# Hybrid short-convolution and RWKV-7 layer on one core: another planner for the instruction order, and rows scaled inside their transposing product

## The chip, the cores and the metric

One core of one Trainium2 chip. The metric is the device time of one execution in microseconds (us). Engines: PE (TensorE, with its weight loads shown apart as PEld), DVE (VectorE), ACT (ScalarE), POOL (GpSimd) and SP (SyncE, used here to issue DMAs). Each engine works through its own queue in order.

## The reference

One layer on 2048 prompt tokens and 8 x 8 sample tokens, with 1024 columns in float32:

```python
xn = rms_norm(x, norm_g)                 # x * rsqrt(mean(x*x) + eps) * g
p = xn @ w_in
pc, pr = p[..., :CONV_COLS], p[..., CONV_COLS:]
# conv branch: u = C*h, width-3 causal conv, y_conv = B * z * silu(G)
pr = pr + mu_shift * (pr_prev - pr)      # token shift; r, k, v, wl, al, gr are its columns
# per head: S_t = S_{t-1} diag(w_t) + (S_{t-1} (-kk_t)) (kk_t*a_t)^T + v_t k_t^T ;  o_t = S_t r_t
new_shift = xn[:, -1]
y = jnp.concatenate([y_conv, y_rwkv], axis=-1) @ w_out
return x + y, new_conv, new_shift, s_fin   # a final RMSNorm follows
```

Outputs are the normalised rows, the last two conv rows, the last normalised input row of each sequence (`shift_p`, `shift_s`) and the 64 x 64 state of each of the 8 heads.

## The kernel before

The 2048 prompt tokens are worked through in two halves of 1024 tokens (the sample tokens ride with the first). A half is cut into three blocks of 256, 384 and 384 tokens; the first block of the first half has 330 columns because of the sample tokens. Eight heads make four pairs, so there are eight steps, s = 0 to 7, in the loop behind L930: half and pair are `divmod(s, 4)`.

`xprep` (L211) prepares a half. It loads rows of 128 tokens, squares them on ACT for the sum, takes a reciprocal root on DVE, and multiplies each row by its factor and by the norm weight in one DVE instruction (`stt`, L120, with `grow`, the weight spread over all partitions). The third row tile of blocks 1 and 2 takes ACT and POOL (L265) instead. Then PE transposes 128 x 128 squares (L286; the sample rows in L279), and each result is split into a rounded part `xh` (ACT) and the rest `xl` (DVE, L207). `xprep(0)` stands at the head, `xprep(1)` in step 3. The rows of outputs `shift_s` and `shift_p` are stored from the scaled rows.

`project` makes the columns of one weight tile for all three blocks: per block 24 matmuls (8 slices of 128, each as wh·xh, wh·xl, wl·xh) into a PSUM tile "pj", of which there are two, then an evacuation by ACT or DVE. In the first half the weights are split by ACT and POOL and saved to DRAM (`wsp`), in the second they are loaded from there by POOL's queue.

A step has these stages. `rwkv_pair` projects k, r, v and the gate and derives from them, by products with constant matrices (PSUM tiles "ax") and DVE work, the per-chunk operands L, bk, AB. `inverse` (L640) inverts the 64 x 64 triangular matrices of all 16 chunks: a substitution of 31 dependent DVE pairs, a transposition through DRAM, then back substitution with 32 x 32 matmuls (PSUM tile "cx") between DVE and ACT copies into `na` (L680, L687). `wkv` then runs 16 chunks of 64 tokens one after the other. Per chunk, `ca` gets L times the state `sv`; DVE copies it to `xs` (L741); `ca` gets AB times xs; DVE scales it to `u` (L751); `cb` gets bt times u; and DVE forms the next state `sv` from cb (L120). Beside the chain, "oo" collects the output. `conv_group` has four projections of its own and the convolution. After the steps, `out_tile` multiplies 17 row tiles by the output weights (48 matmuls each into pj).

Which instruction stands where in each engine's queue is not written in the code: the Tile scheduler takes the program, with its order as priority, through a model of the machine, and lets each engine take the first ready instruction of the model. So the projections of `conv_group` and of the next step fill the places where the chain waits in that model. Tile pools limit how far it goes ahead: two pj tiles, two of each weight tile, four of hp, seven of t. Once made, the order is fixed: an engine whose next instruction waits does not pass it.

Of the kernel before, what the change touches and what calls it, by code (L numbers as in the profile page):

```python
# [36 lines left out]
C_MASK, C_SMASK, C_SCM, C_SCS, C_BM = 0, 128, 256, 640, 704  # L37
NMASK = 712

P_MU, P_KK, P_KA, P_RK, P_LG, P_LB, P_W0, P_A0, P_CW = 0, 17, 21, 25, 29, 33, 37, 41, 45  # L40
NPRM = 57


def constants():
# [43 lines left out]
def trunk_kernel(ctx, tc, I, O):  # L88
# [27 lines left out]
    def copy(out, in_, scale=1.0, bias=0.0):  # L116
        act.activation(out=out, in_=in_, func=AF.Copy, scale=scale, bias=bias)  # L117

    def stt(out, in0, scalar, in1, op0=ALU.mult, op1=ALU.mult, eng=dve):
        eng.scalar_tensor_tensor(out=out, in0=in0, scalar=scalar, in1=in1, op0=op0, op1=op1)  # L120
# [23 lines left out]
    def rowtile():  # L144
        return T("half", [128, HALF + SAMP], "la0", 1)[:, :D]
# [59 lines left out]
    def split(hi, lo, src, eng=dve):  # L205
        copy(hi, src)
        eng.tensor_tensor(out=lo, in0=src, in1=hi.bitcast(F32), op=ALU.subtract)  # L207
# [1 line left out]
    WR = T("w", [128, KT, 128], "wr", 1)  # L209

    def xprep(hf):  # L211
        grow = rowtile()
        if hf == 1:
            act.dma_start(out=grow, in_=I["norm_g"].partition_broadcast(128).rearrange("p a d -> p (a d)"))
        if hf == 0:
            act.dma_start(out=cst[:, 0:128], in_=I["consts"][:, 0:128])
        xh, xl = [], []
        stage = [0]

        def staging():  # L220
            stage[0] += 1
            if stage[0] == (5, 3)[hf] or stage[0] == 11:
                return T("half", [128, HALF + SAMP], "la1", 1)[:, :D]
            if stage[0] == 5:
                return WR.rearrange("p k c -> p (k c)")
            if stage[0] == 6 and hf == 0:
                return T("pair", [128, 32, 32], "na", 1).rearrange("p a b -> p (a b)")
            return T("half", [128, 1108], "hp", 4)[:, :D]

        for bl in half_blocks(hf):  # L230
            h = T("xn", [128, KT, bl.cols], f"xh{bl.i}", 1, F32R)
            l = T("xn", [128, KT, bl.cols], f"xl{bl.i}", 1, F32R)
            xh.append(h)
            xl.append(l)
            rows = []
            if bl.samp:
                rows.append((I["x_sample"], SAMP, bl.c0 + 128))
            for i in range(bl.np // 128):
                tok = hf * HALF + bl.p0 + i * 128
                rows.append((I["x_prompt"][tok:tok + 128, :], 128, bl.c0 + i * 128))  # L240
            ss = T("small", [128, 3], "ssx", 2)[:, :len(rows)]
            if bl.samp:
                pool.memset(ss, 1.0)
            xts = []
            for j, (src, n, o) in enumerate(rows):
                xt = staging()[:n]
                sync.dma_start(out=xt, in_=src)
                junk = l[:n, :, o:o + 128]
                if hf == 1:
                    junk = T("ch", [128, KT, 128], "c2", 4, BF16)  # L250
                act.activation(out=junk, in_=xt.rearrange("p (k c) -> p k c", k=KT), func=AF.Square,
                               accum_out=ss[:n, j:j + 1])
                xts.append(xt)
            if bl.samp:
                sync.dma_start(out=grow, in_=I["norm_g"].partition_broadcast(128).rearrange("p a d -> p (a d)"))
                sr = T("small", [128, 144], "sub", 1)[:, :KT * NB].rearrange("p (k b) -> p k b", k=KT)
                act.dma_start(out=sr, in_=I["state_shift"])
                load_params()
            dve.tensor_scalar(out=ss, in0=ss, scalar1=1.0 / D, scalar2=RMS_EPS, op0=ALU.mult, op1=ALU.add)
            r = rsqrt(ss, len(rows), 128, "n")  # L260
            for j, xt in enumerate(xts):
                n = rows[j][1]
                if bl.i and j == 2:
                    copy(xt, xt, scale=r[:n, j:j + 1])
                    pool.tensor_tensor(out=xt, in0=xt, in1=grow[:n], op=ALU.mult)  # L265
                else:
                    stt(xt, xt, r[:n, j:j + 1], grow[:n])
            if bl.samp:
                pool.memset(h[:, :, 72:74].bitcast(F32), 0.0)
                pool.memset(l[:, :, 72:74].bitcast(F32), 0.0)  # L270
                hv = h[:, :, 0:72].rearrange("p k (b j) -> p k b j", j=9)
                lv = l[:, :, 0:72].rearrange("p k (b j) -> p k b j", j=9)
                split(hv[:, :, :, 0], lv[:, :, :, 0], sr)
                xt = xts.pop(0)
                rows.pop(0)
                pool.dma_start(out=O["shift_s"], in_=xt[7:SAMP:8, :])
                ps = AX([128, KT, SAMP])
                for k in range(KT):
                    pe.transpose(out=ps[:, k, :], in_=xt[:, k * 128:(k + 1) * 128], identity=ident[:SAMP, :SAMP])  # L279
                split(hv[:, :, :, 1:9], lv[:, :, :, 1:9], ps.rearrange("p k (b j) -> p k b j", j=8))  # L280
            for xt, (_, _, o) in zip(xts, rows):
                for q in range(2):
                    ps = AX([128, 4, 128])
                    for k in range(4):
                        kk = q * 4 + k
                        pe.transpose(out=ps[:, k, :], in_=xt[:, kk * 128:(kk + 1) * 128], identity=ident)  # L286
                    split(h[:, q * 4:q * 4 + 4, o:o + 128], l[:, q * 4:q * 4 + 4, o:o + 128], ps)
            if hf == 1 and bl.i == 2:
                act.dma_start(out=O["shift_p"], in_=xts[-1][127:128, :])
        return xh, xl  # L290

    wsp = dram.tile([33, 2, 128, KT, 128], F32, name="wsp")

# [638 lines left out]
    for s in range(8):  # L932
        hf, p = divmod(s, NPAIR)
        first = []
        if p == 0:
            la = [T("half", [128, HALF + SAMP], f"la{i}", 1, F32R) for i in range(2)]

            def la_block(bl):
                t = tmp()[:, :bl.nt]
                ts = slice(bl.t0, bl.t0 + bl.nt)  # L940

                def after():
                    act.activation(out=t[0:64], in_=t[0:64], func=AF.Tanh)
                    for i, hs in heads():
                        hi, lo = la[i][hs, ts], la[i][64 - 64 * i:128 - 64 * i, ts]
                        copy(hi, t[hs])
                        dve.tensor_tensor(out=lo, in0=t[hs], in1=hi.bitcast(F32), op=ALU.subtract)

                return t, after

            first.append((CONV_COLS + 3 * CW, shifter(hf, 12, la_block)))
            if s == 0:
                load_masks()
        S = Pair(hf, p)
        run(rwkv_pair(S, xs, la, *first))
        if s == 3:
            run(conv_group(xs, hf, p))
            xs = xprep(1)
        run(inverse(S))
        wkv(S)  # L960
        if s != 3:
            run(conv_group(xs, hf, p))
# [17 lines left out]
def layout(inputs):  # L980

    import numpy as np

    def cols(name):
        return np.asarray(inputs[name]).reshape(-1, 128).T

    a = {n: np.asarray(inputs[n]) for n in inputs}
    r = {
        "consts": constants()[0],
        "masks": constants()[1],  # L990
        "params": np.concatenate([cols(n) for n in ("mu_shift", "k_k", "k_a", "r_k", "lnx_g", "lnx_b", "w0", "a0",
                                                    "conv_w")], axis=1),
        "w_da": np.concatenate([np.tile(a[n][0].reshape(64, NPAIR, 128).transpose(1, 0, 2), (1, 2, 1))
                                for n in ("w_dec2", "w_a2")], axis=2),
        "state_conv": a["state_conv"].reshape(NB * 2, 4, 128).transpose(2, 1, 0),
        "state_shift": a["state_shift"].reshape(NB, KT, 128).transpose(2, 1, 0),
        "state_wkv": a["state_wkv"].reshape(NB, NPAIR, 2, HD, HD).transpose(1, 2, 4, 0, 3).reshape(
            NPAIR, 128, NB, HD),
        "w_in": a["w_in"].reshape(KT, 128, -1, 128).transpose(2, 1, 0, 3),
        "w_out": a["w_out"][0],  # L1000
        "norm_g": a["norm_g"],
        "final_norm_g": a["final_norm_g"],
        "x_prompt": a["x_prompt"][0],
        "x_sample": a["x_sample"].reshape(SAMP, D),
    }
    return {n: np.ascontiguousarray(v) for n, v in r.items()}
# [22 lines left out]
```

## Time and profile before

| | us |
|---|---|
| median of 3 runs | 1621.16 |
| lowest and highest run | 1619.57, 1629.75 |
| profiled execution, its own time | 1613.0 |
| its span in the profile | 1610.9 |
| PE busy in it | 1512.1 |

The mean granted PE clock of that execution is 0.969 of full speed. The profile is a record of that one execution: start and duration of instructions on every engine, inferred releasers of waits, and the granted clock. A row of the timeline may join several records (x4); a matmul of two heads stands as x2 or x4. "Idle before" is the engine's time without work ahead of that instruction. [...]

### The profile page before, as it was taken

The page shows a single profiled execution, that of the slowest core. Times are in us where ns is not written, and L with a number is a line of the kernel's source. Part 1 is how long each engine was busy: PE and PEld are TensorE (multiplying, and loading weights), DVE is VectorE, ACT ScalarE, POOL GpSimd, SP SyncE. Part 2 cuts the span into 40 slices and gives each one's busy share as a digit, 9 for nine tenths or more (in the row PEclk, how much of TensorE's full clock was granted, in tenths as well). Part 3 has the DMA queues.
Part 4 walks back from the last instruction along what each step waited for, and adds up shares of the span by engine and source line. Part 5 has one row for each costly group of instructions (what it writes and reads, how often), then busy time and mean ns, then how long its engine had stood idle before and what let it go on. Part 6 is the DMA issues. An engine that isn't in the chain of part 4 may idle for free.

```text
span 1610.9 us, 29335 instructions
## 1 busy us (share of the span) xinstructions
PE 1512.1 (94%) x11088; PEld 1265.4 (79%) x11088; DVE 1011.3 (63%) x3101; ACT 616.2 (38%) x1591; POOL 289.6 (18%) x395
## 2 busy tenths in 40 slices
PE   4999999999999999989999999999999999899997
PEld 4989778887788777877789678877897788567885
DVE  6377458765687458784586358545864578466544
ACT  6443346324542354344541354135313543342221
POOL 3134103311133112320022002200220022000000
PEclk9989999899999998999999899999999999899999
DMA  7323412342043213441124112411241145414441
GB/s 241 118 83 110 137 49 74 108 122 78 20 136 113 95 50 112 140 125 61 36 73 125 42 36 66 135 39 37 77 127 38 34 118 155 133 62 137 143 137 53
DMA packets 121967, 151.90 MB, mean 94 GB/s; under 512 B 62617, under 2 KB 86681, under 8 KB 121826
## 3 DMA queue, kind: packets, MB, share of 16 engines
q1 hardware_dynamic: 107024, 104.53, 21.2%
q0 software_dynamic: 9536, 34.64, 6.8%
q10 hardware_dynamic: 5266, 10.86, 1.9%
q8 instruction: 88, 1.44, 0.4%
q14 instruction: 53, 0.43, 0.1%
HBM read 92.60 MB, written 57.35 MB: 93 GB/s over the span
## 4 chain that ended last, share of the span: by engine, by line
PE 63%; DVE 23%; issue 5%; DMA 5%; ACT 2%; POOL 1%; SPq 1%; ACTq 0%; DVEq 0%; POOLq 0%
PE pj L129 41%; PE ca L129 5%; PE ax L129 5%; DVE sub L123 5%; PE cb L129 4%; DVE xi L123 4%; DVE hp L123 2%; PE oo L129 2%; PE cx L129 2%; DVE hp L120 1%; PE cx L703 1%; DVE bk L123 1%; DVE t L120 1%; DMA dx<-xi 1%; DMA AB<-dx 1%
## 5 line engine op out<-in xcount | busy, mean ns | idle before, releaser
L129 PE MATMUL pj<-xh,wh 128*128 128x384 f32 (+3 forms) x1856 | 655.4, 354 | 18.0 <-DVE hp L123 13.8
L129 PE MATMUL pj<-xl,wh 128*128 128x384 f32 (+3 forms) x1856 | 652.8, 352 | 2.7 <-POOL xl L207 2.1
L129 PE MATMUL pj<-xh,wl 128*128 128x384 f32 (+3 forms) x1856 | 650.9, 351 | 0.8 <-DMA wl<-wsp 0.8
L129 PEld LDWEIGHTS pj<-xh,wh 128*128 128x128 f32 x1856 | 356.7, 192 | 50.1 <-DVE hp L123 11.5
L129 PEld LDWEIGHTS pj<-xl,wh 128*128 128x128 f32 x1856 | 356.8, 192 | 31.7 <-POOL xl L207 3.0
L129 PEld LDWEIGHTS pj<-xh,wl 128*128 128x128 f32 x1856 | 355.8, 192 | 27.3 <-issue 1.7
L117 ACT ACTIVATE tS<-sv,wc 64x64 f32<-64x64 f32 x256 | 88.0, 344 | 114.8 <-DVE sv L120 94.2
L207 POOL TENSOR_TENSOR wl<-wr,wh 128x512 fp32r<-128x512 f32 x66 | 87.8, 1342 | 193.4 <-ACT wh L117 190.0
L120 DVE SCALAR_TENSOR_TENSOR sv<-cb,wc,tS 64x64 f32<-64x64 f32 x240 | 68.0, 283 | 62.6 <-PE cb L129 56.1
L129 PE MATMUL ax<-L,bk 64*128 64x128 f32 x528 | 79.1, 298 | 20.9 <-DVE bk L123 11.2
L129 PEld LDWEIGHTS ax<-L,bk 64*128 64x128 f32 x528 | 66.1, 197 | 37.9 <-issue 23.6
L123 DVE TENSOR_TENSOR sub<-xi,na 128x126 f32<-128x126 f32 (+22 forms) x248 | 81.5, 329 | 16.5 <-DMA na<-dn 9.7
L117 ACT ACTIVATE t<-pj,prm 128x384 f32<-128x384 f32 (+3 forms) x170 | 68.8, 433 | 54.5 <-PE pj L129 53.4
L751 DVE TENSOR_SCALAR u<-ca,Q 128x64 f32<-128x64 f32 x128 | 36.2, 283 | 82.3 <-PE ca L129 82.1
L531 POOL TENSOR_TENSOR bk<-t,t 64x384 f32<-64x384 f32 (+2 forms) x56 | 58.3, 1041 | 155.3 <-ACT t L503 72.9
L123 DVE TENSOR_TENSOR xi<-xi,sub 128x126 f32<-128x126 f32 (+22 forms) x248 | 77.6, 313 | 7.1
L117 ACT ACTIVATE wh<-wr 128x512 fp32r<-128x512 f32 x66 | 40.5, 626 | 92.0 <-PE pj L129 73.1
L129 PEld LDWEIGHTS ca<-sv,L 128*64 128x64 f32 x528 | 43.3, 134 | 37.2 <-DVE sv L120 12.8
L129 PE MATMUL ca<-sv,L 128*64 128x64 f32 x528 | 67.8, 245 | 0.1
L741 DVE COPY xs<-ca 128x64 f32<-128x64 f32 x128 | 28.7, 224 | 60.4 <-PE ca L129 50.6
L298 POOL DMA_DIRECT2D wh<-wsp x33 | 18.6, 565 | 254.1 <-PE pj L129 216.7
L123 DVE TENSOR_TENSOR hp<-pj,hp 128x512 f32<-128x512 f32 (+1 forms) x34 | 23.4, 689 | 62.6 <-PE pj L129 62.2
(207 smaller groups left out, 2057.4 us busy)
## 6 DMA issues: line engine op xcount, KB each, us to landing
wr<-in_w_in SPq DMA_DIRECT2D x66, 256.0 KB, 3.7
wsp<-wh SPq DMA_DIRECT2D x33, 512.0 KB, 3.1
wsp<-wl SPq DMA_DIRECT2D x33, 512.0 KB, 3.5
wh<-wsp POOLq DMA_DIRECT2D x33, 512.0 KB, 3.6
wl<-wsp POOLq DMA_DIRECT2D x33, 512.0 KB, 4.8
hp<-in_x_prompt SPq DMA_DIRECT2D x28, 512.0 KB, 4.1
la<-yd SPq DMA_DIRECT2D x16, 512.0 KB, 4.0
out_y_p<-hp ACTq DMA_DIRECT2D x16, 512.0 KB, 2.6
```

Of the source, the lines that this page charges most:

```text
L117: act.activation(out=out, in_=in_, func=AF.Copy, scale=scale, bias=bias)
L120: eng.scalar_tensor_tensor(out=out, in0=in0, scalar=scalar, in1=in1, op0=op0, op1=op1)
L123: dve.tensor_tensor(out=out, in0=in0, in1=in1, op=op)
L129: pe.matmul(out, lhsT=lhsT, rhs=rhs, start=start, stop=stop)
L207: eng.tensor_tensor(out=lo, in0=src, in1=hi.bitcast(F32), op=ALU.subtract)
L298: pool.dma_start(out=wh, in_=wsp[col, 0])
L531: pool.tensor_tensor(out=S.bk[bl.i][hs, chs, h, :], in0=ta[hs, a:a + n].rearrange("p (c j) -> p c j", j=64), in1=wi[hs, a:a + n].rearrange ...
L703: pe.transpose(out=pb[:, i, :], in_=S.bk[bi][:, ca + i].rearrange("p a t -> p (a t)"), identity=ident)
L741: dve.tensor_copy(out=xs_, in_=px)
L751: dve.tensor_scalar(out=u, in0=pu, scalar1=S.Q[:, q:q + 1], scalar2=None, op0=ALU.mult)
```

## The change

It has three parts. First, the Tile context gets `schedule_with_timeline_sim=True`: the scheduler's model of the machine is its detailed timing model, and the order on every engine comes out another way. Second, `xprep` no longer scales rows. DVE makes a diagonal matrix `dg` of the row factors (identity times r, 128 x 128 per row tile), and PE multiplies the row tile, as stationary operand, with it, slice by slice for all row tiles of a block. The product is the transposed, scaled slice. The norm weight, now one value per partition (8 more columns of the parameters, `P_NG`), is applied as ACT rounds to `xh` and as DVE forms `xl`. Third, `shift_rows`, called in step 0, loads the nine rows that the two shift outputs need and normalises them apart.

```diff
-NPRM = 57
+NPRM = 65
...
     def xprep(hf):
-        grow = rowtile()
...
             r = rsqrt(ss, len(rows), 128, "n")
-            for j, xt in enumerate(xts):
-                n = rows[j][1]
-                if bl.i and j == 2:
-                    copy(xt, xt, scale=r[:n, j:j + 1])
-                    pool.tensor_tensor(out=xt, in0=xt, in1=grow[:n], op=ALU.mult)
-                else:
-                    stt(xt, xt, r[:n, j:j + 1], grow[:n])
+            dg = tmp()
+            offs, o = [], 0
+            for j, (_, n, _) in enumerate(rows):
+                dve.tensor_scalar(out=dg[:n, o:o + n], in0=ident[:n, :n], scalar1=r[:n, j:j + 1], scalar2=None,
+                                  op0=ALU.mult)
+                offs.append((o, n))
+                o += n
...
-            for xt, (_, _, o) in zip(xts, rows):
-                for q in range(2):
-                    ps = AX([128, 4, 128])
-                    for k in range(4):
-                        kk = q * 4 + k
-                        pe.transpose(out=ps[:, k, :], in_=xt[:, kk * 128:(kk + 1) * 128], identity=ident)
-                    split(h[:, q * 4:q * 4 + 4, o:o + 128], l[:, q * 4:q * 4 + 4, o:o + 128], ps)
+            for k in range(KT):
+                tag, nb = (("ax", 2), ("ax", 2), ("cx", 1), ("oo", 1))[k % (4 if hf == 0 else 3)]
+                ps = PS([128, bl.np], tag, nb)
+                for i, (xt, (o, n)) in enumerate(zip(xts, offs)):
+                    mm(ps[:, i * 128:(i + 1) * 128], xt[:, k * 128:(k + 1) * 128], dg[:, o:o + n])
+                hk = h[:, k, bl.c0:bl.c0 + bl.np]
+                copy(hk, ps, scale=pcol(P_NG, k))
+                stt(l[:, k, bl.c0:bl.c0 + bl.np], ps, pcol(P_NG, k), hk.bitcast(F32), ALU.mult, ALU.subtract)
         return xh, xl
+
+    def shift_rows():
...
+        sync.dma_start(out=xt[0:NB], in_=I["x_sample"][7:SAMP:8, :])
+        sync.dma_start(out=xt[NB:n], in_=I["x_prompt"][SEQ - 1:SEQ, :])
...
+        act.activation(out=junk, in_=xt, func=AF.Square, accum_out=s)
+        dve.tensor_scalar(out=s, in0=s, scalar1=1.0 / D, scalar2=RMS_EPS, op0=ALU.mult, op1=ALU.add)
+        r = rsqrt(s, 1, n)
+        for q in range(2):
+            m = slice(q * 512, (q + 1) * 512)
+            g = T("ch", [128, 512], "c2", 4)[:n]
+            sync.dma_start(out=g, in_=I["norm_g"].partition_broadcast(n).rearrange("p a d -> p (a d)")[:, m])
+            stt(xt[:, m], xt[:, m], r, g)
+        act.dma_start(out=O["shift_s"], in_=xt[0:NB])
+        act.dma_start(out=O["shift_p"], in_=xt[NB:n])
...
-    with tile.TileContext(nc) as tc:
+    with tile.TileContext(nc, schedule_with_timeline_sim=True) as tc:
         trunk_kernel(tc, I, O)
```

The order on PE in one chunk of `wkv`, in step 5, before (ca, cb and oo are the chain's PSUM tiles, sv the state, bt and AB its operands, pj_12202 a projection of 256 columns):

```order
L129 MATMUL cb_11167<-sv_11149,bt_11148 64x64 x2
L129 MATMUL pj_12202<-xl_1193_7387,wh_12198 128x256
L129 MATMUL pj_12202<-xh_1192_7386,wl_12199 128x256
L129 MATMUL ca_11166<-xs_11250,AB_1738_10345 64x64 x2
L129 MATMUL pj_12202<-xh_1192_7386,wh_12198 128x256
L129 MATMUL pj_12202<-xl_1193_7387,wh_12198 128x256
L129 MATMUL pj_12202<-xh_1192_7386,wl_12199 128x256
L129 MATMUL pj_12202<-xh_1192_7386,wh_12198 128x256
L129 MATMUL cb_11167<-u_11259,bt_11148 64x64 x2
L129 MATMUL oo_11165<-u_11259,AB_1738_10345 64x64 x2
```

Every link here has projections behind it: two before the product of xs, four before that of u. A chunk of step 5 on PE after the change:

```order
L129 MATMUL ca_11386<-sv_11306,L_1761_10414 64x64
L129 MATMUL oo_11384<-sv_11306,L_1761_10414 64x64
L129 MATMUL ca_11386<-sv_11306,L_1764_10417 64x64
L129 MATMUL oo_11384<-sv_11306,L_1764_10417 64x64
L129 MATMUL cb_11387<-sv_11306,bt_11305 64x64 x2
L129 MATMUL ca_11386<-xs_11413,AB_1767_10420 64x64 x2
L129 MATMUL cb_11387<-u_11422,bt_11305 64x64 x2
L129 MATMUL oo_11384<-u_11422,AB_1767_10420 64x64 x2
```

A whole chunk, from the state sv to oo from u, now stands without a projection; they have moved to other chunks and out of the chain.

The second place is on PE in the back substitution of step 5, before (each cx of x12 is one product for the six chunks of block 1, the first operand of the next comes from DVE and ACT):

```order
L129 MATMUL pj_12142<-xl_1206_7442,wh_12107 128x384
L129 MATMUL cx_11082<-na_11049,AB_1739_10346 32x32 x12
L129 MATMUL pj_12142<-xh_1205_7441,wl_12108 128x384
L129 MATMUL pj_12142<-xh_1205_7441,wh_12107 128x384
L129 MATMUL pj_12142<-xl_1206_7442,wh_12107 128x384
L129 MATMUL pj_12142<-xh_1205_7441,wl_12108 128x384
L129 MATMUL pj_12142<-xh_1205_7441,wh_12107 128x384
L129 MATMUL cx_11097<-AB_1739_10346,na_11049 32x32 x12
L129 MATMUL pj_12142<-xl_1206_7442,wh_12107 128x384
```

Five pj stand between the first and the second product. The same place on PE after the change (pj_12402 is a projection of the first block, 256 columns):

```order
L129 MATMUL cx_11156<-na_11123,AB_1767_10420 32x32 x12
L129 MATMUL pj_12402<-xh_1209_7436,wh_12367 128x256
L129 MATMUL pj_12402<-xl_1210_7437,wh_12367 128x256
L129 MATMUL cx_11171<-AB_1767_10420,na_11123 32x32 x12
L129 MATMUL pj_12402<-xh_1209_7436,wl_12368 128x256
L129 MATMUL pj_12402<-xh_1209_7436,wh_12367 128x256
L129 MATMUL pj_12402<-xl_1210_7437,wh_12367 128x256
```

The projections between the first and the second product of this block are two instead of five; behind the second there are 22 in a row before the next product, where before there were five between each and the next.

## Rows read from the trace of the kernel before

**Rows 1.** Page, parts 1 and 2: busy time by engine, PE's forty slices

```profile
PE 1512.1 (94%) x11088; PEld 1265.4 (79%) x11088; DVE 1011.3 (63%) x3101; ACT 616.2 (38%) x1591; POOL 289.6 (18%) x395
...
PE   4999999999999999989999999999999999899997
```

**Rows 2.** Windows: span, PE busy (x count), granted clock, DMA share, GB/s

```profile
961.95:1063.03 101.08, 94.02 (x687) 0.97 0.30 85
1063.03:1120.28 57.25, 57.25 (x532) 1.00 0.13 44
1120.28:1225.10 104.82, 96.68 (x699) 0.95 0.31 85
```

**Rows 3.** Windows, the chunk chain, instructions of tile pj alone

```profile
1063.03:1120.28 57.25, 35.26 (x150) 1.00 0.13 44
```

**Rows 4.** Timeline, a filled chunk: start us, us, engine, line, operation

```profile
1093.45 0.60 DVE L120 SCALAR_TENSOR_TENSOR sv<-cb,wc,tS 64x64 f32<-64x64 f32 x2 [0.77 <-PE cb L129]
...
1093.93 0.33 PE L129 MATMUL ca<-sv,L 128*64 128x64 f32 x2
...
1095.84 0.34 PE L129 MATMUL pj<-xh,wh 128*128 128x384 f32 x1
1096.01 0.33 PE L129 MATMUL pj<-xl,wh 128*128 128x384 f32 x1
...
1096.73 0.60 DVE L120 SCALAR_TENSOR_TENSOR sv<-cb,wc,tS 64x64 f32<-64x64 f32 x2 [0.77 <-PE cb L129]
```

**Rows 5.** Timeline, a chunk with little beside it

```profile
227.07 0.60 DVE L120 SCALAR_TENSOR_TENSOR sv<-cb,wc,tS 64x64 f32<-64x64 f32 x2 [0.89 <-PE cb L129]
...
227.65 0.41 PE L129 MATMUL ca<-sv,L 128*64 128x64 f32 x3
...
228.16 0.22 DVE L741 COPY xs<-ca 128x64 f32<-128x64 f32 x1 [0.48 <-PE ca L129]
...
228.43 0.33 PE L703 MATMUL cx<-cst,bk 128*128 128x128 f32 x1
...
228.69 0.33 PE L129 MATMUL ca<-xs,AB 64*64 64x64 f32 x4
...
229.07 0.28 DVE L751 TENSOR_SCALAR u<-ca,Q 128x64 f32<-128x64 f32 x1 [0.69 <-PE ca L129]
...
229.58 0.33 PE L129 MATMUL cb<-u,bt 64*64 64x64 f32 x4
...
229.75 0.28 PE L129 MATMUL oo<-u,AB 64*64 64x64 f32 x4
...
230.03 0.60 DVE L120 SCALAR_TENSOR_TENSOR sv<-cb,wc,tS 64x64 f32<-64x64 f32 x2 [0.68 <-PE cb L129]
```

**Rows 6.** Waits of PE: total us, times, longest us

```profile
PE cx L129 <- DVE na L680: 14.6, 6, 5.2
PE pj L129 <- DVE hp L123: 13.8, 11, 2.5
```

**Rows 7.** Windows, columns as in rows 2, around a fall of the clock

```profile
276.00:281.60 5.60, 4.07 (x30) 1.00 0.61 209
281.60:292.00 10.40, 10.01 (x33) 0.53 0.34 113
292.00:302.00 10.00, 10.00 (x62) 0.97 0.02 3
```

**Rows 8.** Timeline of PE, six records at either clock level

```profile
286.04 1.65 PE L129 MATMUL ax<-L,bk 64*128 64x128 f32 x6
...
303.18 0.90 PE L129 MATMUL ax<-L,bk 64*128 64x128 f32 x6 [0.84 <-DVE L L123]
```

**Rows 9.** Costliest groups of the head, 0 to 40 us: busy us, mean ns, idle before

```profile
L120 DVE SCALAR_TENSOR_TENSOR hp<-hp,nwyn,la 128x1024 f32<-128x1024 f32 x5 | 8.2, 1660 | 0.1
```

**Rows 10.** Instructions of line L286: ns min/median/max, first and last start us

```profile
L286 PE MATMUL ax<-cst,wr x8: 270/272/273, 709.1 to 710.1; 128*128 128x128 f32 x8
```

**Rows 11.** Windows of the head, columns as in rows 2

```profile
0.00:40.00 40.00, 20.07 (x104) 1.00 0.72 243
```

More of the change, by code (lines that the diff above doesn't have):

```diff
@@ L38 @@
 NMASK = 712
-P_MU, P_KK, P_KA, P_RK, P_LG, P_LB, P_W0, P_A0, P_CW = 0, 17, 21, 25, 29, 33, 37, 41, 45
-NPRM = 57
+P_MU, P_KK, P_KA, P_RK, P_LG, P_LB, P_W0, P_A0, P_CW, P_NG = 0, 17, 21, 25, 29, 33, 37, 41, 45, 57
+NPRM = 65
 def constants():
@@ L211, in xprep @@
     def xprep(hf):
-        grow = rowtile()
-        if hf == 1:
-            act.dma_start(out=grow, in_=I["norm_g"].partition_broadcast(128).rearrange("p a d -> p (a d)"))
         if hf == 0:
@@ L254, in xprep @@
             if bl.samp:
-                sync.dma_start(out=grow, in_=I["norm_g"].partition_broadcast(128).rearrange("p a d -> p (a d)"))
                 sr = T("small", [128, 144], "sub", 1)[:, :KT * NB].rearrange("p (k b) -> p k b", k=KT)
@@ L274, in xprep @@
                 xt = xts.pop(0)
-                rows.pop(0)
-                pool.dma_start(out=O["shift_s"], in_=xt[7:SAMP:8, :])
+                offs.pop(0)
                 ps = AX([128, KT, SAMP])
                 for k in range(KT):
-                    pe.transpose(out=ps[:, k, :], in_=xt[:, k * 128:(k + 1) * 128], identity=ident[:SAMP, :SAMP])
-                split(hv[:, :, :, 1:9], lv[:, :, :, 1:9], ps.rearrange("p k (b j) -> p k b j", j=8))
-            for xt, (_, _, o) in zip(xts, rows):
-                for q in range(2):
-                    ps = AX([128, 4, 128])
-                    for k in range(4):
-                        kk = q * 4 + k
-                        pe.transpose(out=ps[:, k, :], in_=xt[:, kk * 128:(kk + 1) * 128], identity=ident)
-                    split(h[:, q * 4:q * 4 + 4, o:o + 128], l[:, q * 4:q * 4 + 4, o:o + 128], ps)
@@ L288, in xprep @@
-            if hf == 1 and bl.i == 2:
-                act.dma_start(out=O["shift_p"], in_=xts[-1][127:128, :])
-        return xh, xl
+                    mm(ps[:, k, :], xt[:, k * 128:(k + 1) * 128], dg[:SAMP, 0:SAMP])
+                sx = T("ch", [128, KT, SAMP], "c2", 4)
+                tt(sx, ps, prm[:, P_NG:P_NG + KT].unsqueeze(2).to_broadcast([128, KT, SAMP]), ALU.mult)
+                split(hv[:, :, :, 1:9], lv[:, :, :, 1:9], sx.rearrange("p k (b j) -> p k b j", j=8))
+            for k in range(KT):
[6 more added lines that the diff above has]
+                stt(l[:, k, bl.c0:bl.c0 + bl.np], ps, pcol(P_NG, k), hk.bitcast(F32), ALU.mult, ALU.subtract)
@@ new lines, in xprep @@
+        return xh, xl
+    def shift_rows():
+        n = NB + 1
+        xt = T("pair", [128, 32, 32], "na", 1).rearrange("p a b -> p (a b)")[:n]
+        sync.dma_start(out=xt[0:NB], in_=I["x_sample"][7:SAMP:8, :])
+        sync.dma_start(out=xt[NB:n], in_=I["x_prompt"][SEQ - 1:SEQ, :])
+        junk = T("ch", [128, D], "c2", 4, BF16)[:n]
+        s = T("small", [128, 1], "ss", 2)[:n]
+        act.activation(out=junk, in_=xt, func=AF.Square, accum_out=s)
[8 more added lines that the diff above has]
+        act.dma_start(out=O["shift_p"], in_=xt[NB:n])
@@ L958, in trunk_kernel @@
             xs = xprep(1)
+        if s == 0:
+            shift_rows()
         run(inverse(S))
@@ L991, in layout @@
         "params": np.concatenate([cols(n) for n in ("mu_shift", "k_k", "k_a", "r_k", "lnx_g", "lnx_b", "w0", "a0",
-                                                    "conv_w")], axis=1),
+                                                    "conv_w", "norm_g")], axis=1),
         "w_da": np.concatenate([np.tile(a[n][0].reshape(64, NPAIR, 128).transpose(1, 0, 2), (1, 2, 1))
```

## Prediction

> **What bounds the kernel now.** I read the page's busy times and slices first [rows 1]. TensorE (PE) is busy 1512.1 of 1610.9 us, VectorE (DVE) 63%, and PE's slices are full but for the first and some eights. So PE's own queue sets the time, and the change can act only through PE's idle time (about 1610.9 - 1512.1 = 99 us, some 20 of them in the head), through PE's clock, or through the number and price of its instructions.
>
> Next, one step by stage [rows 2]. From the end of one pair's chunk chain to the end of the next pass 101.08 + 57.25 us here: outside the chain 101.08 us with 94.02 busy, 7.1 idle, clock 0.97; chunks 1 to 15 in 57.25 us without idle, clock 1.00; the next outside stretch 104.82 with 8.1 idle, clock 0.95. Inside the chain PE is covered only because 150 projection matmuls (tile pj) stand between the links [rows 3].
>
> How much cover that is, two chunks show, each measured from one state update sv to the next. The filled one [rows 4] takes 1096.73 - 1093.45 = 3.28 us with seven pj (two of them shown); pj follow each other at 1096.01 - 1095.84 = 0.17 us, so seven are 1.21 us and the chunk without them 2.07. The lightly filled one [rows 5] takes 230.03 - 227.07 = 2.96 us: the chain goes by sv, ca, the copy xs, ca, u, cb, sv, and each hop is a handover between PE and DVE. Few pj and transposes (cx) lie in it, in the gaps of the chain.
>
> PE's waits come from outside the chain [rows 6]: back substitution (cx for DVE's na) 14.6 us, and projections waiting for DVE to empty their PSUM bank (pj for hp) 13.8 us.
>
> Last the clock [rows 7]. [...] At the lower level six records of an ax matmul last 1.65 us against 0.90 [rows 8].
>
> **The order inside the chain.** In the new PE order most chunks hold no pj. Counted over the listing: in steps 0 to 3 chunks 1 to 7 and 10 to 13, in steps 4 to 6 chunks 1 to 6 and 9 to 13, in step 7 chunks 2 to 8 and 11 to 12, together 86 chunks in 16 stretches. The same projections stand in batches before, between and after these stretches; outside the chain about as many as before. A bare chunk puts up waits that were covered: ca on xs waits for DVE's copy, cb on u for DVE's scaling, the next ca on sv for DVE's update; behind each stand only later links, and the pj that could run are queued behind those. What does one last? The lightly filled chunk bounds it at 2.96. Its first hop (sv to ca) is 0.58 us, in the filled chunk 1093.93 - 1093.45 = 0.48; that leaves 2.86. In the hop from xs to ca (0.53) a cx transpose stands in PE's queue just ahead of the waiting ca (228.43, 0.26 us earlier), which I put at 0.1: 2.76. For the lower bound I take 0.2 us more off, the rest of what stands ahead of waiting matmuls: 2.55. Against 2.07 for a filled chunk without its pj, 2.75 is 0.68 more: 86 x 0.68 = **+58** (bounds 0.48 and 0.89: 41 to 77).
>
> **Outside the chain.** Batches moved there into other places: between the products of the back substitution there are now 2 and 22 pj in the first block, where five stood after each product. That covers the 14.6 us wait of rows 6, and projections begun elsewhere cover part of the 13.8. Of the 7 to 8 us idle per step I take half: 8 x 3.5 = **-28** (bounds 0 and -60, all of it). What is late next there is DVE's evacuation of the two pj banks. The clock outside was 0.97 and 0.95 [rows 2], that is 3.0 and 5.2 us lost per step, 33 in eight; the thin stretches that bring it are the ones now filled, so two thirds go: **-22** (bounds 0 and -33).
>
> **The clock inside the chain.** A bare chunk, without the pj and transposes of rows 5, has PE busy for about 0.6 (ca 0.41, with two oo beside and behind it) + 0.33 + 0.33 (cb, and ca on xs) + 0.45 (cb on u to the end of oo, 229.58 to 230.03) = 1.7 of 2.75 us, 62%, with half-width matmuls; the stretch before the fall in rows 7 had 4.07 of 5.60, 73%. So I expect the clock to fall some 5 us into a stretch, two chunks. 86 - 16 x 2 = 54 chunks then run at the lower level. Of their 1.7 us of PE about two thirds (1.1 us) I take to grow by the ratio 1.65 to 0.90 of rows 8, the rest being fixed delay: 2.0 for 1.1, 0.9 more each, 54 x 0.9 = **+49** (bounds 0, and 54 x 1.4 = 76 if all 1.7 us grow so). [...] The batch behind each stretch starts at the lower level too. In rows 7 this cost 10.4 x 0.47 = 4.9 us, but there with waits in between; an unbroken batch is nearer to the row behind it (10 us at 0.97, so 0.3 lost), so I take 1 us: 16 x 1 = **+16** (bounds 5 and 78).
>
> **The second row preparation.** It loses the stt that scale rows (1.66 us each on DVE, [rows 9]), and one such row on ACT and POOL. Its 64 transposes, one every (710.1 - 709.1) / 7 = 0.14 us [rows 10], become matmuls with diag(r) in float32, which leave two records each; six records of a comparable product last 0.90 [rows 8], 0.30 for two. So 64 x 0.16 = **+10** on PE, which is full there (bounds 0 and 20). The evacuation keeps one ACT and one DVE pass per element; beside 37% free DVE time I cost it at nothing, and if that cover goes, its few passes of 0.6 us are late by 2 us at most.
>
> **The head.** PE is busy 20.07 of its first 40 us [rows 11], so 72 transposes that become matmuls hide there. On the path three DVE scalings leave (1.66 us each), and three small diag(r) products come: **-5** (bounds 0 and -10).
>
> **The shift rows.** Nine rows more are loaded, squared, scaled and stored in step 0, with 3 to 4 SP loads and two ACT stores; the DMA share is 0.30 and nothing on PE reads them. **+2** (bounds 0 and 5) for DVE and ACT time ahead of the first substitution. The weight loads are moved with their projections; with DMA at 0.3 and SP and POOL mostly waiting, I cost that at nothing; if that cover goes, a batch of projections waits for its weights, and the price is that of (c) below.
>
> **Sum.** 1613.0 (profiled execution; span 1610.9) + 58 - 28 - 22 + 49 + 16 + 10 - 5 + 2 = 1693. The median of the runs shown is 1621.2, 0.5% above that execution; I leave that in the range. A measurement of this kernel can tell about 1% from no change, so faster is below 1605 and slower above 1637.
>
> **Rivals.**
> (a) The clock holds. Then 49 and 16 go: 1693 - 65 = 1628, no change. For it: the head had a clock of 1.00 with PE busy 20.07 of 40 us [rows 11], and the lightly filled chunk ran at full clock. Against it: rows 7, and that a stretch of five to seven bare chunks, 14 to 19 us, is longer than any thin one now.
> (b) Faster: the cover outside is what counts. If the idle time outside goes whole (-60), the spells at the lower clock too (-33), the clock holds in the chain, and a bare chunk is 2.55 (+41), the time is 1613 - 60 - 33 + 41 + 10 - 5 + 2 = 1568. It turns where 86 chunks give back 60 + 33 - 7 = 86 us, at 1.0 us each: a mean bare chunk of 3.07 us, clock and batches included. For it: 28 us of waits in rows 6 have exactly this cover. Against: in the chain there was no idle at all to win.
> (c) More than my forecast: the new order also puts DVE's evacuations of the batched projections between the links of chunks 14 and 15. If each of eight steps loses 6 us by it, and the batches 3 us instead of 1, 1693 + 48 + 32 = 1773.
> (d) The new order does not do what the listing says: excluded, since PE takes its queue in order.
>
> **How the numbers follow.** Forecast 0.55, own range 1640 to 1750; (a) 0.20; (b) 0.18; (c) 0.07. Leaving out half of (c) and the fast end of (b), the range is 1590 to 1760. Slower: 0.55 + 0.07 + a fifth of (a), 0.66. Same: 0.15 of (a). Faster: 0.18, and 0.01 of (a).
>
> **What would show it.** Right: chunks without pj of 2.7 to 2.9 us at full clock and some 3.6 later in the same stretch; clock below 0.9 in the windows of chunks 3 to 7; less idle outside (3 to 4 us per step); the waits for na gone. Wrong: clock 1.00 through a bare stretch, or a bare chunk under 2.4 us, or outside stretches still of 100 us with the same waits. A total at 1628 with bare chunks at full clock is rival (a), one under 1600 is (b).

## The result: slower, by twice what was forecast

| | before | after |
|---|---|---|
| median of the runs, us | 1620.37 (4 runs) | 1774.14 (4 runs) |
| ratio, with its 95% interval | | 1.0937 [1.0886, 1.0988] |
| profiled execution, us | 1613.0 | 1770.29 |
| its span, us | 1610.9 | 1768.5 |
| mean granted clock | 0.969 | 0.878 |

The direction was right. The size was not: 1693 was forecast and 1760 was the upper end of the range. The two profiled spans differ by 157.6 us, where the sum had 80.

The page's busy times of after, against [rows 1]:

```profile
PE 1591.5 (90%) x11224; PEld 1370.5 (77%) x11224; DVE 1001.9 (57%) x3136; ACT 621.7 (35%) x1605; POOL 279.6 (16%) x390
...
PEclk9999877997689877999789977997899689996879
```

PE's busy time rose by 79.4 us and its idle time by 1768.5 - 1591.5 - (1610.9 - 1512.1) = 78.2 us. The clock row has a seven or a six in each of the eight steps. Before, it had nines and eights only:

```profile
PEclk9989999899999998999999899999999999899999
```

Windows of PE (span, busy, clock, DMA share, GB/s) for a step that answers to [rows 2]: outside, chain, outside, then the chain's projections alone, as in [rows 3]. The busy time is the union over a stretch and the clock its mean; the records of the granted clock in the traces of before and after have two values, 1.0 (full clock) and 0.5 of it (the lower level):

```profile
1101.81:1188.66 86.85, 83.05 (x646) 1.00 0.32 97
1188.66:1270.17 81.51, 72.45 (x575) 0.79 0.11 33
1270.17:1358.64 88.47, 84.70 (x645) 0.98 0.32 95
```

```profile
1188.66:1270.17 81.51, 29.00 (x134) 0.79 0.11 33
```

The chain now takes 81.51 us in place of 57.25, with 9.1 idle where there was none, at a clock of 0.79. Outside it is 14 to 16 us shorter, with about 4 idle in place of 7 to 8. These two can't be compared by themselves, because work moved between them: the trace has some 450 records of ax matmuls in the eight chains, where before had 32. Projections, as a whole, did not move out of the chains: 1148 of their records stand there, 1125 before, but now in 35 chunks in place of all 120. PE's idle time can be compared all the same. The last line of the table of windows over the eight chains is, for before and then after:

```profile
sum 461.63, PE 461.63; mean PE 57.70
```

```profile
sum 698.79, PE 619.35; mean PE 77.42
```

And over the nine stretches outside, before and then after:

```profile
sum 1149.27, PE 1050.47; mean PE 116.72
```

```profile
sum 1069.71, PE 972.17; mean PE 108.02
```

PE's idle time in the chains went from 0 to 79.4 us; outside it stayed (98.8 and 97.5). So the loss has two halves: 79 us of new idle time in the chain, and 79 us by which PE is busy longer. The projections are the same (5568 records in both); the row preparation is not, and the experiments tell its share.

A bare chunk on the timeline of after at full clock (PE and DVE, weight loads left out):

```profile
1191.05 0.33 PE L129 MATMUL cb<-u,bt 64*64 64x64 f32 x4 [0.39 <-DVE u L766]
...
1191.50 0.60 DVE L120 SCALAR_TENSOR_TENSOR sv<-cb,wc,tS 64x64 f32<-64x64 f32 x2 [0.50 <-PE cb L129]
...
1191.83 0.33 PE L129 MATMUL ca<-sv,L 128*64 128x64 f32 x2 [0.33 <-DVE sv L120]
...
1192.52 0.23 DVE L756 COPY xs<-ca 128x64 f32<-128x64 f32 x1 [0.42 <-PE ca L129]
...
1193.18 0.28 DVE L766 TENSOR_SCALAR u<-ca,Q 128x64 f32<-128x64 f32 x1 [0.43 <-PE ca L129]
1193.52 0.33 PE L129 MATMUL cb<-u,bt 64*64 64x64 f32 x4 [0.39 <-DVE u L766]
```

From cb to cb it is 2.47 us (2.75 was forecast). The first hop, from sv to ca, is 0.33 us, where [rows 4, 5] had 0.48 and 0.58 with a projection ahead. In two such chunks PE is busy 3.50 of 4.94 us, and two later ones in the same step, at the lower level, take half a microsecond more each (windows; one of the later two holds a transpose):

```profile
1191.05:1195.99 4.94, 3.50 (x49) 1.00 0.01 3
1233.52:1239.49 5.97, 5.11 (x49) 0.50 0.00 0
```

Of the 128 chunks 120 lie between the first and the last of a step; 85 of these are bare, and 56 of the bare ones have a mean clock of 0.86 or less. Of those without any other matmul, 22 at full clock last 2.49 us on average and 22 wholly at the lower level 3.07.

The batches behind the stretches show the clock best. Chunk 14 of steps 4, 5 and 6 has the same instructions, 39 projection matmuls among them, and three times (windows):

```profile
1075.99:1089.59 13.60, 12.92 (x85) 0.77 0.05 16
1245.11:1257.95 12.84, 12.16 (x85) 0.82 0.05 17
1413.09:1430.01 16.92, 16.24 (x84) 0.59 0.04 13
```

Times its clock each gives 10.5, 10.5 and 10.0 us: these batches paid for the lower clock in full. Two projections in a row, at the lower level in the third and at full clock in the chunk behind the second (timelines):

```profile
1416.34 0.41 PE L129 MATMUL pj<-xh,wl 128*128 128x256 f32 x1
1416.55 0.41 PE L129 MATMUL pj<-xh,wh 128*128 128x256 f32 x1
```

```profile
1259.94 0.33 PE L129 MATMUL pj<-xh,wl 128*128 128x384 f32 x1
1260.12 0.33 PE L129 MATMUL pj<-xh,wh 128*128 128x384 f32 x1
```

256 columns follow at 0.21 us there, and 384 columns at 0.18 here. Summed over the windows of all 35 filled chunks, span times (1 - clock) is 62 us.

PE's waits, against [rows 6] (us in total, times, longest):

```profile
PE cb L129 <- DVE u L766: 30.8, 68, 1.4
PE ca L129 <- DVE sv L120: 20.2, 70, 0.7
...
PE pj L129 <- DVE t L120: 12.4, 14, 1.6
...
PE pj L129 <- DVE hp L123: 5.2, 5, 1.7
PE pj L129 <- DVE v L120: 4.7, 9, 0.7
...
PE cx L129 <- DVE na L702: 2.7, 5, 0.8
```

The 14.6 us wait for na (L680, now L695) is gone, as forecast; the 2.7 are those of the second na, formed at L687 before, which took 1.6. The chain's own links took its place. PE's waits for DVE to empty a projection's bank did not shrink: t, hp and v are 22.3 us here, and hp and t were 13.8 + 2.8 before.

Last the end, windows from the last chunk on, before and then after, with the waits of PE in it after:

```profile
1454.75:1610.90 156.15, 146.88 (x645) 0.99 0.37 118
```

```profile
1693.87:1768.50 74.63, 48.43 (x204) 0.82 0.20 63
```

```profile
PE pj L129 <- ACT wh L117: 9.4, 1, 9.4
PE cx L881 <- ACT c L875: 7.4, 3, 7.0
```

And the head, against [rows 11]:

```profile
0.00:40.00 40.00, 27.45 (x182) 1.00 0.69 231
```

At the end, before, 633 projection matmuls were still to come behind the last chunk and covered its output steps; now 192 are. PE idles 26.2 us there in place of 9.3.

### The profile page after: what moved, and what is told of

Same layout as the page of the kernel before. It is cut to its first block, busy times and chain, and to the rows that moved or that the text cites. A ratio compares the mean times of both kernels' runs of the same rounds, so it can differ in the third digit from the quotient of the medians.

```text
span 1768.5 us, 29576 instructions
## 1 busy us (share of the span) xinstructions
PE 1591.5 (90%) x11224; PEld 1370.5 (77%) x11224; DVE 1001.9 (57%) x3136; ACT 621.7 (35%) x1605; POOL 279.6 (16%) x390
## 4 chain that ended last, share of the span: by engine, by line
PE 70%; DVE 17%; issue 5%; DMA 4%; ACT 3%; POOL 1%; SPq 1%; DVEq 0%; POOLq 0%; ACTq 0%
PE pj L129 46%; PE ax L129 7%; PE ca L129 5%; PE cb L129 4%; PE oo L129 2%; DVE sub L123 2%; PE cx L129 2%; DVE xi L123 2%; DVE c L120 2%; DVE sv L120 1%; DMA na<-dn 1%; DVE u L766 1%; PE cx L881 1%; PE cx L718 1%; DVE t L120 1%
## 5 line engine op out<-in xcount | busy, mean ns | idle before, releaser
L129 PEld LDWEIGHTS pj<-xh,wh 128*128 128x128 f32 x1856 | 365.3, 197 | 65.6 <-ACT wh L117 13.1
L129 PEld LDWEIGHTS pj<-xl,wh 128*128 128x128 f32 x1856 | 365.5, 197 | 20.2 <-POOL xl L207 2.2
L129 PEld LDWEIGHTS pj<-xh,wl 128*128 128x128 f32 x1856 | 363.9, 196 | 18.7 <-DMA wl<-wsp 0.7
L129 PE MATMUL ca<-sv,L 128*64 128x64 f32 x528 | 88.2, 297 | 25.7 <-DVE sv L120 20.2
L129 PEld LDWEIGHTS ca<-sv,L 128*64 128x64 f32 x528 | 56.9, 172 | 57.2 <-DVE sv L120 36.2
L123 DVE TENSOR_TENSOR sub<-xi,na 128x126 f32<-128x126 f32 (+22 forms) x248 | 73.2, 295 | 36.8 <-DMA na<-dn 30.5
L129 PEld LDWEIGHTS ax<-L,bk 64*128 64x128 f32 x528 | 67.0, 190 | 19.3 <-issue 15.8
L129 PE MATMUL cb<-u,bt 64*64 64x64 f32 x512 | 51.6, 289 | 30.8 <-DVE u L766 30.8
L123 DVE TENSOR_TENSOR AB<-ax,msk 64x384 f32<-64x384 f32 (+2 forms) x88 | 48.8, 554 | 53.5 <-PE ax L129 52.4
L129 PE MATMUL oo<-sv,L 128*64 128x64 f32 x528 | 75.5, 274 | 0.0
L129 PEld LDWEIGHTS cb<-u,bt 64*64 64x64 f32 x512 | 30.9, 165 | 57.5 <-DVE u L766 47.0
```

What stands on the lines that cost most here:

```text
L123: dve.tensor_tensor(out=out, in0=in0, in1=in1, op=op)
L129: pe.matmul(out, lhsT=lhsT, rhs=rhs, start=start, stop=stop)
```

## The experiments

**The order alone, and the code alone.** The first is the kernel before with one line changed, the second the changed kernel with that line put back:

```diff
-    with tile.TileContext(nc) as tc:
+    with tile.TileContext(nc, schedule_with_timeline_sim=True) as tc:
```

> Only the planner's model is changed, rows are prepared as before. Theory (the order, through TensorE's clock and the bare chunks, is the whole loss): 1755 to 1785 us, mean clock 0.87 to 0.89 as after the change, bare chunks of 2.4 to 2.5 us at full clock and about 3.0 at the lower level. Rival (the product with diag(r) or the shift rows carry a good part of the loss): below 1720 us.

Measured: 1771.93 us, ratio to before 1.0951 [1.0907, 1.0996], clock 0.879, both as the theory had them.

> The new row preparation and shift rows, planned with the model of before. Theory: 1610 to 1635 us, clock 0.96 to 0.975, step times as before but for the head and the fourth step. Rival (the product with diag(r) costs what was lost): above 1680 us.

Measured: 1632.79 us, ratio 1.0087 [1.0051, 1.0122], clock 0.963. So the order is the whole loss. The new row preparation and the shift rows cost some 12 us (8 to 20 by the interval) in the old order, and in the new one no cost is seen (1774.14 against 1771.93). The pages' busy times of the order alone and of the code alone:

```profile
PE 1576.1 (89%) x11088; PEld 1352.3 (77%) x11088; DVE 1009.6 (57%) x3101; ACT 617.9 (35%) x1591; POOL 291.1 (16%) x395
```

```profile
PE 1536.2 (94%) x11224; PEld 1288.2 (79%) x11224; DVE 1001.2 (61%) x3136; ACT 618.0 (38%) x1605; POOL 277.1 (17%) x390
```

The order alone, with the same 11088 matmul records as before, keeps PE busy 64 us longer and idle 90 us longer (span 1764.7). Against it the changed kernel, which has the new code planned the same way, has PE busy 15 us more and idle 12 us less.

The trace of the code alone shows the 12 us mostly elsewhere than the forecast had its 10. The stretch with the second row preparation is even shorter than before (137.32 against 140.16 us), but at a higher clock: times its clock it is 134.6 against 130.3, some 4 us more. The stretches ahead of the second and third chains are longer, at a lower clock; why it is lower there is not shown. These are one execution each, and their spans differ by 20.5 us. Windows of the code alone, then of before:

```profile
258.81:381.65 122.84, 114.57 (x761) 0.90 0.35 110
439.76:564.79 125.03, 115.90 (x762) 0.90 0.35 111
624.55:761.87 137.32, 126.41 (x911) 0.98 0.37 113
```

```profile
255.85:372.84 116.99, 110.07 (x761) 0.94 0.36 116
430.90:546.43 115.53, 107.01 (x761) 0.99 0.39 120
606.19:746.35 140.16, 127.24 (x870) 0.93 0.40 121
```

**Idle matmuls, to hold the clock.** If the lower clock makes the loss, and if work in the gaps keeps the clock up, which was an assumption, useless work in the chain should pay for itself. Four bf16 matmuls of 256 columns were put into each prompt chunk of both kernels, into a part of the ca bank that is added for them; nothing reads what they write:

```diff
+            fill = pc[0][:, 4:8].rearrange("p a b -> p (a b)")
+            for _ in range(4 if sample is None else 0):
+                mm(fill, msk[:, 0:128], msk[:, 128:384])
             for h, hs in heads():
                 mm(pu[hs], AB[hs, c, 0:64], xs_[hs])
```

> The changed kernel with four idle bf16 matmuls of 256 columns more in each of the 128 prompt chunks, ahead of the product of xs, into an unused part of the ca bank; nothing reads them. Theory (the lower clock is most of the loss): they take 4 x 0.11 us but hold the clock, so 1640 to 1700 us although there is more work, granted clock in the chain stages 0.95 or more. Rival (the order's waits and evacuations themselves are the loss): the added work only costs, 1775 to 1830 us, whatever the clock does.

> The kernel before with the same four idle matmuls per chunk. There the clock in the chain is 1.00 already, so by both theories they only cost: 128 x 0.3 to 0.5 us, 1655 to 1690 us. If it came out at or under 1620, the idle matmuls would help by something other than the clock, and the run with them on the changed kernel could not be read as the clock's price.

Measured: 1810.04 us for the changed kernel, 1670.45 for the one before. The control came as expected (50 us, 0.39 per chunk). The other missed the theory's range and lies in the rival's. It did not try the theory, whose condition was a clock of 0.95 or more: the clock did not hold. Windows of two of its chains, which have 0.76 to 0.87 in all:

```profile
1208.75:1309.80 101.05, 93.28 (x683) 0.78 0.12 37
1393.39:1490.38 96.99, 89.18 (x685) 0.82 0.18 52
```

The distance between the two kernels was 140 us, against 154 without idle matmuls.

**Ten in place of four**, five ahead of the product of xs and five behind it.

> The changed kernel with ten idle bf16 matmuls of 256 columns in each prompt chunk, five ahead of the product of xs and five behind it; some 80 chunks still hold no projection. The four of the run before were too few to hold the clock. Theory (in the chain the lower clock is most of the loss): with ten the granted clock in the chain stages is 0.95 or more, and the time stands only 20 to 60 us above the kernel before with the same ten, so 1750 to 1810 us. Rival (waits and evacuations of the new order are the loss): 140 to 170 us above it, 1870 to 1920 us, with the clock up or not.

> The kernel before with the same ten idle matmuls per chunk: the four cost 50 us, 0.39 per chunk, so ten cost 128 x 0.98 = 125 us by both theories: 1725 to 1770 us, clock in the chain 1.00.

Measured: 1842.14 us (ratio to before 1.1356 [1.1316, 1.1397]) and 1750.72 us (1.0802 [1.077, 1.0834]), the control as expected. The chains' clock was now 0.91 to 1.00, in half of the eight a little short of what was expected, and the distance 91 us: outside both ranges, between theory and rival.

**Seven, in the gaps of the chain only**, in chunks 1 to 7 and 10 to 13, most of which are bare, and where the clock falls:

```diff
+            idle = sample is None and q - cb in (1, 2, 3, 4, 5, 6, 7, 10, 11, 12, 13)
+            for _ in range(3 if idle else 0):
+                mm(fill, msk[:, 0:128], msk[:, 128:384])
             for h, hs in heads():
                 mm(px[hs], L[h][:, c, 0:64], sv[:, i, h, :])
...
+            for _ in range(2 if idle else 0):
+                mm(fill, msk[:, 0:128], msk[:, 128:384])
             for h, hs in heads():
                 mm(pu[hs], AB[hs, c, 0:64], xs_[hs])
+            for _ in range(2 if idle else 0):
+                mm(fill, msk[:, 0:128], msk[:, 128:384])
```

> The changed kernel with seven idle bf16 matmuls of 256 columns in chunks 1 to 7 and 10 to 13 only, spread over the three gaps of the chain (three ahead of ca on sv, two ahead of ca on xs, two behind it), where PE waits anyway; the batch chunks have none. 84 chunks still hold no projection. Theory (the lower clock in the bare chunks and in the batches behind them is most of the loss): granted clock in the chain stages 0.95 or more, batch chunks of 12 us in place of 13 to 17, bare chunks about 2.8 us throughout, and the whole 1680 to 1745 us, faster than the changed kernel with 616 matmuls more. Rival (the order's waits and evacuations): the idle matmuls only cost, 1790 to 1830 us.

> The kernel before with the same seven idle matmuls in the same eleven chunks of a step. No gap is free there and the clock is up, so by both theories they cost 88 x 0.6 to 0.7 us: 1665 to 1690 us.

Measured: 1745.88 us (ratio to before 1.0776 [1.072, 1.0832]), 28 us faster than the changed kernel although it has 616 matmuls more, and 1677.94 us for the control (1.0343 [1.0302, 1.0383]), as expected. The distance is 68 us, less than half of 154. The rival's range is left far off; the theory's is missed by 1 us. Windows of three chains and of the end:

```profile
846.90:933.91 87.01, 78.36 (x698) 1.00 0.14 44
1017.53:1098.96 81.43, 74.85 (x673) 0.98 0.15 46
1188.17:1280.58 92.41, 83.06 (x723) 0.98 0.14 41
...
1660.04:1746.80 86.76, 77.30 (x344) 0.97 0.28 91
```

The 28 us need care, since the planner, given more work, also placed some projections otherwise. Up to the first chunk of step 7 this run and the changed kernel are equal (1577.83 and 1578.61 us into the span, with 5128 and 5107 records of projections done), while its bare chunks there last about 3.10 in place of 2.47 us at full clock. For 77 chunks that is some 48 us paid and got back, by the clock. The price of 0.63 us a chunk is also the control's (58 us for 88 chunks, 0.66), so the smaller distance does not come from idle matmuls that were cheaper here. The gain shown lies behind that point, where 332 projection matmuls are left for the end and PE idles 9.5 us there in place of 26.2.

The busy times of PE in the profiled executions put the pairs side by side. The pages of four, ten and seven idle matmuls, each time the changed kernel and then its control:

```profile
PE 1648.5 (91%) x11736; PEld 1398.9 (77%) x11736; DVE 1008.8 (56%) x3136; ACT 625.4 (35%) x1605; POOL 275.1 (15%) x390
PE 1567.8 (94%) x11600; PEld 1305.1 (78%) x11600; DVE 1009.4 (60%) x3101; ACT 618.5 (37%) x1591; POOL 288.4 (17%) x395
PE 1675.0 (91%) x12504; PEld 1420.7 (77%) x12504; DVE 1004.0 (54%) x3136; ACT 622.9 (34%) x1605; POOL 274.5 (15%) x390
PE 1646.1 (94%) x12368; PEld 1372.8 (78%) x12368; DVE 1020.4 (58%) x3101; ACT 616.8 (35%) x1591; POOL 287.0 (16%) x395
PE 1597.5 (91%) x11840; PEld 1349.2 (77%) x11840; DVE 999.3 (57%) x3136; ACT 621.6 (36%) x1605; POOL 275.8 (16%) x390
PE 1574.1 (94%) x11704; PEld 1314.3 (78%) x11704; DVE 1022.3 (61%) x3101; ACT 618.8 (37%) x1591; POOL 288.9 (17%) x395
```

| idle matmuls | clock in the chains, changed kernel | span, us more | PE busy, us more | PE idle, us more |
|---|---|---|---|---|
| none | 0.74 to 0.82 | 158 | 79 | 78 |
| four | 0.76 to 0.87 | 140 | 81 | 59 |
| ten | 0.91 to 1.00 | 95 | 29 | 66 |
| seven, in the gaps | 0.85 to 1.00 | 70 | 23 | 46 |

Where the clock rose, PE's extra busy time fell from about 80 to between 23 and 29 us; where it did not, it stayed. That share of the loss, some 50 us, goes with the clock. The new idle time stayed for the most part, and of the 32 us that it lost in the last pair 17 lie at the end, where the planner had left more projections.

No run beat the kernel before.

## Why the prediction was right in sign and wrong in size

Its terms can be set beside idle and busy time of PE:

| term of the sum | forecast, us | measured, us |
|---|---|---|
| idle in the chain | +58 | +79 |
| idle outside, and the head | -28 - 5 | -1 |
| clock and PE's work: 49 + 16 - 22 + 10 + 2 | +55 | +79 |
| sum | +80 | +158 |

All three were too low, by 21, 32 and 24 us, the second most.

**The order inside the chain.** The mechanism is right: 85 bare chunks, PE waiting for u and sv. Its price was wrong in both numbers, and both errors raised it. A bare chunk at full clock is 2.47 us, not 2.75. And the 2.07 it was set against came from one chunk: the chain of [rows 2] has some 77 pj of 384 and 73 of 256 columns, at 0.17 and 0.11 us, so (57.25 - 13.1 - 8.0) / 15 = 2.4 us is the mean without pj. In the forecast's own terms a bare chunk at full clock thus costs less than 0.1 us, not 0.68. What came is idle time, because in the chains before PE used those gaps: 58.6 us in the 85 bare chunks (summed over their windows), 0.69 each. That this meets the +58 is luck. The other 20.8 us stand in chunks that hold batches, which the term left out.

**Outside the chain.** This step failed most: -33 us of idle time were forecast with the head, -1 came. The wait for na went, and the head's idle time fell by 7.4 us (27.45 of 40 us busy against 20.07). In the four stretches ahead of chains 5 to 8 the idle time fell from 35.3 to 15.8 us, as in the step shown above. But in the three ahead of chains 2 to 4 it rose from 28.4 to 32.1, and the end lost 16.9 us: work drawn forward was missing there as cover (of 441 projection matmuls 302 now stand ahead of the eighth chain and 139 in it). That was readable from the order (192 projections left, not 633), and no term had it. The -22 for the clock did not come either: outside, span times (1 - clock) over nine windows is 56 us after and 50 before.

**The clock inside the chain.** Right: it falls, in 56 bare chunks (54 forecast). The estimate of 0.9 us for each was high for most: chunks without other matmuls show 0.5 to 0.6, since the wait for u did not stretch (0.39 us ahead of cb at 1191.05, at full clock, and at 1236.50, at the lower level). The eight chunks that hold two transposes pay more; they last 3.56 us at the lower level. The term for the batches was the mis-sized one: 1 us each, 16 in all, from the row at 0.97, where the windows show 62 us in 35 chunks. [Rows 7] had the right price beside it, 4.9 us for a stretch at 0.53. I set it aside as one with waits in between, but the row does not say so: PE is busy 10.01 of its 10.40 us. The 5.6 us ahead of it were misread too, as a likeness of bare chunks: they hold mostly projections one behind another and one wait of 1.5 us. With 56 x 0.5 = 28, 62 and 6 outside, the clock is worth some 96 us by this estimate; in the run with the order alone, PE's busy time rose by 64 only. What gave back the rest is not shown. The rows point to fewer changes between projections and other matmuls (635 against 1367): a bare chunk at full clock has PE busy 1.75 us, where the mean chunk before, less its projections, has 2.4. No run tried this alone.

**The rest.** Row preparation and shift rows: +7 forecast for all of it; 12 measured in the old order, mostly not at the place named, and none seen in the new order. Rival (a), a clock that holds, is out by the trace. Rival (b) is out: its condition was a mean bare chunk below 3.07 us with batches included, and the bare ones alone average 3.2. Rival (c), more than the forecast, is what came, though not by the evacuations that it named: in the chains PE waited 4.7 us for them (v), where the rival had 48. The chains' clock was 0.74 to 0.82 without idle matmuls, 0.76 to 0.87 with four of them in one gap of every chunk, and 0.85 to 1.00 with seven spread over the gaps.

Open: why this planner draws projections together into a few chunks. In step 5 the next pair's r projections stand ahead of the chain now (DVE empties their banks from 1156.8 us on, the chain begins at 1188.66), while before they filled its first ten chunks (1075.7 to 1098.7 us in the chain from 1063.03 on). No run tried to hold them back.

## What to carry to other kernels

Where independent matmuls filled the gaps of the serial chain, they paid twice here: they used the waits (PE idle 0 us in the eight chains before, 79.4 after), and TensorE's clock stayed up for the dense work behind them (1.00 in the chains before, 0.74 to 0.82 after). When an instruction order changes, count the dense work per link of each chain and also behind the last one, and price a batch that follows a thin stretch at the lower clock (here 12.84 to 16.92 us at 0.82 to 0.59, where span times clock is 10.0 to 10.5). Take the price of a link from a mean over the stage, not from one chunk.

## What the runs showed of the hardware that was not expected

A serial chunk lost little by the lower clock (2.47 us at full clock, 2.98 at the lower level from 1233.52 us on, with nothing else in either), a batch nearly all of it (12.84 us at 0.82, 16.92 at 0.59). Added useless matmuls were free in one run: 616 of them made this order no slower up to its eighth step (1577.83 us to its first chunk against 1578.61; PE's busy time rose by 6 us in all, where in the kernel before they added 62), and 512 placed in one gap of every chunk, where the clock stayed at 0.76 to 0.87 in the chains, made it 36 us slower.
